# First-layer memory attention of a two-layer decoder: four-pass products replaced by three one-pass products of exact parts, with their splits, transfers and places moved

## The chip, the cores and the metric

The kernel runs on one core of a Trainium2 chip. The metric is device time in microseconds (us) of one execution; before the change the median of three runs is 2042.42 us (2042.41 to 2042.49). The span in the profile is the part of an execution between its first and last recorded instruction.

## The reference, cut to what matters

256 positions, width 2048, two layers. Layer 0 (mixer A) runs chunked gMLP gating beside a 4-head cross-attention into 256 memory tokens. The part that the change touches is that attention of layer 0:

```python
def memory_attention(q_m, mem, g_mem, w_mem_kv):
    q = q_m.reshape(B, S, MEM_HEADS, MEM_HEAD_DIM)          # 256 x 4 x 128
    kv = rmsnorm(mem, g_mem) @ w_mem_kv
    k = kv[..., :MEM_W].reshape(B, M, MEM_HEADS, MEM_HEAD_DIM)
    v = kv[..., MEM_W:].reshape(B, M, MEM_HEADS, MEM_HEAD_DIM)
    s = jnp.einsum('bshd,bmhd->bhsm', q, k) * (MEM_HEAD_DIM ** -0.5)
    p = jax.nn.softmax(s, axis=-1)
    return jnp.einsum('bhsm,bmhd->bshd', p, v).reshape(B, S, MEM_W)
# layer 0:
z = h @ w_in_a[0]          # 2048 x 3584: 1536 gate u, 1536 gate v, 512 memory queries
main = spatial_gating(z[..., :G_W], z[..., G_W:2 * G_W], ...)
x = x + concatenate([main, memory_attention(z[..., 2 * G_W:], ...)]) @ w_out[0]
```

## The kernel before, in words

**Exact parts.** Almost every product is made from two parts of each operand. A part is a `float32r` tile: the high part is the value rounded by a ScalarE copy, the low part is value minus high part, made by VectorE. Three one-pass matmuls (high x high, high x low, low x high) give the product. A few small products were left as plain `float32` matmuls, among them the scores and outputs of memory attention in both layers (`memory_scores`, `memory_out`). The trace records each such `float32` matmul as two instructions.

**Weights.** `chunk` loads a 128 x 2 x 512 piece of weights (512 KB) into a `raw` buffer on SyncE's queue (SP), then makes `whi` on ScalarE (ACT) and `wlo` on VectorE (DVE). There are four buffers of each. `gemm_fm` works on two chunks at a time, called a pair below: for both chunks all products with `whi` (L179, L180), then all with `wlo` (L182); 96 one-pass matmuls of 128x256 in all, the last 32 of them L182. After a pair, the hooks of its two chunks run: `hooks[c]` is a list of functions for chunk c. `gemm_tm` takes chunks one by one and multiplies with `whi`, `wlo`, `whi` in turn.

**Start.** `start` first makes the keys and values of layer 0 (names `kT`, `mv`, accumulated in four PSUM banks), then two GEMMs for layer 1: a `gemm_fm` of 8 chunks (hooks[0]) for the keys, and a `gemm_tm` of 8 chunks (hooks[1]) for the values. Between them, hooks evict layer 0's keys (`ek`) and values (`ev`), and `operand(h)` makes the parts of two blocks of the operand `xhl` for layer 0, h = 0 to 7. In `start`, program order is kept on PE, ACT, DVE and SP.

**Layer A.** In order: three `gemm_tm` for the v gates; one `gemm_fm` for the memory queries `qm` (with the spatial gates, L715, in hooks 4 to 7); three `gemm_fm` for the u gates, c = 0, 1, 2 with 8 chunks each, here written c0#0 to c2#7; then `w_out`. Scores of heads 0, 1 run after c0#3, those of heads 2, 3 after c0#5. The softmax result (`pm`, one 128 x 2048 tile) must be transposed. `Turn.squares` does 32x32 blocks on DVE into `small` (half of the tile at a time; the second half, `squares(8, 8)`, after c1#1), and 16 DMAs (`Turn.place`, 64 KB each) carry the blocks to their places in `pm`. `Pending.ask` spreads these 16 over the chunk loads that follow: after a load is issued on SP, `pending.some()` issues the number of places listed for it. For c = 1 and 2 program order is kept on SP. So a load behind a place on SP is not issued before that place has been. `memory_out` follows after c2#5, and `w_out` takes the four heads' blocks (12 to 15) first.

**What sets the order elsewhere.** Outside the blocks named, a scheduler sets the order in each engine's queue; PE is kept busy by the four buffers, which let loads and splits run ahead of it.

Of the kernel before, what the change touches and what calls it, by code (L numbers as in the profile page):

```python
# [101 lines left out]
class Kernel:  # L102
# [341 lines left out]
    def start(self):  # L444
# [4 lines left out]
        self.kT = [pool.tile([P, MH, S], F32, name=self.uid("kT")) for pool in (self.mk, self.cp)]  # L449
        self.mv = [pool.tile([P, 2, MW], F32, name=self.uid("mv")) for pool in (self.mk, self.cp)]  # L450
        self.rt = self.cp.tile([P, 2], F32, name="rt0")
        self.rb = self.tmp(self.cp, [P, S], "rbc", 2)
        with tc.tile_pool(name="st", bufs=1) as st:
# [48 lines left out]
            for k in range(NB):  # L502
# [29 lines left out]
                for f in hooks.get(k, ()):  # L532
# [9 lines left out]
                {  # L542
                    0: [lambda: [f() for f in late], call(operand, 5)], 1: [call(operand, 6)] + sums(self.x, xparts, 0), 2: [call(operand, 7)] + sums(self.x, xparts, 1),
                    3: sums(self.x, xparts, 2), 4: sums(self.x, xparts, 3), 5: [call(ask, "x", xparts)],
                    6: [lambda: nc.sync.dma_start(out=self.cT, in_=t["conv"]), call(columns, "x", self.rt)],
                    7: [call(rows, "x", self.rb)],
                },
# [5 lines left out]
    def memory_scores(self, l, h, q, pool, p):  # L553
        nc = self.nc
        acc = self.psum()
        for sb in range(2):
            nc.tensor.matmul(  # L557
                acc[:, sb * S : (sb + 1) * S], q[:, sb * P : (sb + 1) * P], self.kT[l][:, h, :], start=True, stop=True
            )
# [12 lines left out]
    def memory_out(self, l, h, pT, hl):  # L572
        nc, v = self.nc, self.mv[l]
        o = self.psum()
        for mb in range(2):
            nc.tensor.matmul(o[:, :S], v[:, mb, h * P : (h + 1) * P], pT[:, mb * S : (mb + 1) * S], start=mb == 0, stop=mb == 1)  # L576
        self.split(hl[:, GH + h, :], o[:, :S])


# [93 lines left out]
    def layer_a(self):  # L673
        nc, t, tc = self.nc, self.t, self.tc
        w, xhl, rt, rb = t["w_in_a"][0], self.xhl, self.rt, self.rb
        x = lambda k: xhl[:, k, :]
        ks = list(range(NB))
        with ExitStack() as ctx:
            la = ctx.enter_context(tc.tile_pool(name="la", bufs=1))
            vn = la.tile([P, 2, GW], F32, name="vn")  # L680
            vs = la.tile([P, 2, 3], F32, name="vs")

            zhooks = ({2: [lambda: self.rope_angles(la)]}, {4: [self.rope_tables]}, {})
            for c in range(3):

                def evz(tb, acc):
                    cols = slice(c * 512, (c + 1) * 512)
                    nc.scalar.activation(vn[:, tb, cols], acc, AF.Gelu, scale=rt[:, tb : tb + 1])
                    nc.scalar.activation(acc, vn[:, tb, cols], AF.Square, accum_out=vs[:, tb, c : c + 1])

                self.gemm_tm(self.rows(w, GW + c * 512, 512), NB, 512, x, evz, hooks=zhooks[c])
            vt = la.tile([P, 2], F32, name="vt")
            vr = la.tile([P, 2], F32, name="vr")
            nc.vector.tensor_reduce(vt, vs, AX.X, ALU.add)
            self.rstd(vr, vt, GW, self.cp, "rt")
            for tb in range(2):
                nc.vector.tensor_scalar(vn[:, tb, :], vn[:, tb, :], vr[:, tb : tb + 1], None, ALU.mult)

            qm = la.tile([P, MH, S], F32, name="qm")
            wT = la.tile([P, GH, P], F32, name="wT")  # L700
            bb = la.tile([P, GH, P], F32, name="bb")

            def spatial_weights():
                nc.sync.dma_start(out=bb, in_=t["b_sp"][0].rearrange("(o g) t -> o g t", o=1).to_broadcast([P, GH, P]))
                nc.sync.dma_start(out=wT, in_=t["w_sp"])
                for g in range(0, GH, 4):
                    mask = self.keep.rearrange("p (o t) -> p o t", o=1).to_broadcast([P, 4, P])
                    nc.vector.tensor_tensor(wT[:, g : g + 4, :], wT[:, g : g + 4, :], mask, ALU.mult)
# [12 lines left out]
            def eq(b, acc):
                self.scaled(qm[:, b : b + 2, :], acc, rb)
# [5 lines left out]
            pm, small = (la.tile([P, MH * 512], F32, name=name) for name in ("pm", "small"))  # L728
            turned = Turn(nc, pm, small, 4 * MH)

            def scores(h):
                view = pm[:, 512 * h : 512 * (h + 1)].rearrange("p (m a c) -> p a m c", m=2, a=2)
                self.memory_scores(0, h, qm[:, h, :], la, view)

            def out(h):
                self.memory_out(0, h, pm[:, 512 * h : 512 * (h + 1)], hl)

            each = lambda f, *hs: [lambda h=h: f(h) for h in hs]
            mhooks = {2: each(scores, 0, 1), 4: each(scores, 2, 3) + [lambda: turned.squares(0, 8)]}, {0: [lambda: turned.squares(8, 8)]}, {5: each(out, *range(MH))}
            for c in range(3):  # L740

                def eu(b, acc):
                    g = 4 * c + b
                    u = self.tmp(la, [P, 2, S], "u", 2)
                    self.scaled(u, acc, rb)
                    nc.scalar.activation(u, u, AF.Gelu)
                    u4 = u.rearrange("p g (n t) -> p g n t", n=2)
                    v4 = vn[:, :, g * P : (g + 2) * P].rearrange("p n (g t) -> p g n t", g=2)
                    nc.vector.tensor_tensor(u4, u4, v4, ALU.mult)
                    self.split_pair(hl[:, g : g + 2, :], u)  # L750

# [353 lines left out]
```

## Time and profile before

| | us |
|---|---|
| median of 3 runs | 2042.42 |
| the profiled execution | 2042.17 |
| its span | 2040.5 |
| PE busy | 2030.8 |
| DVE busy | 1362.5 |
| ACT busy | 1043.7 |

The profiled execution took 2042.17 us, 1.67 us more than its span, and lies 0.25 us under the median. PE matmuls are busy in practically the whole span. In the profile, PE is TensorE, `ps<-kT,qm` is a matmul that writes PSUM tile `ps` from `kT` and `qm`; `xN` is a count of instructions, and in the chain of waits a row gives start, duration, what and count. SPq rows are the issuing of DMAs by SyncE. An entry like `[1.90 <-DMA raw]` says that the engine sat idle so long before, and for what.

### The profile page before, as it was taken

Reading aid. Unit: us, or ns where it says so; the run is one execution under the profiler, and the core shown is the slowest. Engines: PE = TensorE matmul, PEld = TensorE weight load, DVE = VectorE, ACT = ScalarE, POOL = GpSimd, SP = SyncE. Lnnn points to the kernel's source line nnn. Section 1 sums busy time; section 2 is a strip of 40 time slices with the busy share of each in tenths; the row PEclk is TensorE's granted clock in tenths of the full one; section 3 lists DMA queues with packets and bytes.
Section 4 is the critical chain, followed back from the end, with each engine's and each line's share of the span. In section 5 each row is a group of like instructions: output and inputs, shape, how many; then the busy total and the mean of one; then the engine's idle time right before and its main releaser. Section 6 shows DMA issues by size and latency. Waiting matters only on the chain.

```text
span 2040.5 us, 38983 instructions
## 1 busy us (share of the span) xinstructions
PE 2030.8 (100%) x16200; PEld 1964.5 (96%) x16200; DVE 1362.5 (67%) x1858; ACT 1043.7 (51%) x1356; POOL 94.4 (5%) x125
## 2 busy tenths in 40 slices
PE   9999999999999999999999999999999999999998
PEld 8889999999999999999999999999988999889997
DVE  6866667767556666457689876777655667656675
ACT  6754644555435554345556674455543555434543
POOL 0000013000000000000052001200000000000000
PEclk9999999999999999999999999999999999999999
DMA  8575855666666666566665564578766666666654
GB/s 311 189 227 175 195 182 186 203 191 193 199 190 194 196 195 197 188 196 192 190 196 178 179 151 157 191 209 217 223 197 192 192 200 188 196 197 186 197 186 154
DMA packets 236753, 396.70 MB, mean 194 GB/s; under 512 B 47776, under 2 KB 54304, under 8 KB 236448
## 3 DMA queue, kind: packets, MB, share of 16 engines
q1 hardware_dynamic: 236288, 393.70, 63.0%
q8 instruction: 126, 2.06, 0.4%
q10 hardware_dynamic: 288, 0.52, 0.1%
q14 instruction: 51, 0.42, 0.1%
HBM read 387.88 MB, written 2.10 MB: 191 GB/s over the span
## 4 chain that ended last, share of the span: by engine, by line
PE 99%; DMA 0%; DVE 0%; issue 0%; ACT 0%; POOLq 0%; POOL 0%; DVEq 0%
PE ps L182 26%; PE ps L179 26%; PE ps L180 26%; PE ps L211 6%; PE ps L212 5%; PE ps L210 5%; DMA raw<-in_w_mem_kv 0%; PE ps L888 0%; PE ps L557 0%; PE ps L576 0%; PE ps L529 0%; PE ps L528 0%; PE ps L531 0%; PE ps L715 0%; PE ps L921 0%; PE ps L890 0%
## 5 line engine op out<-in xcount | busy, mean ns | idle before, releaser
L143 DVE TENSOR_TENSOR wlo<-raw,whi 128x1024 fp32r<-128x1024 f32 (+1 forms) x672 | 819.3, 1235 | 606.2 <-issue 413.7
L142 ACT ACTIVATE whi<-raw 128x1024 fp32r<-128x1024 f32 (+1 forms) x672 | 705.0, 1056 | 785.3 <-PE ps L180 569.9
L179 PE MATMUL ps<-xhl,whi 128*128 128x256 f32 x3264 | 751.2, 276 | 0.0
L180 PE MATMUL ps<-xhl,whi 128*128 128x256 f32 x3264 | 750.4, 276 | 0.0
L179 PEld LDWEIGHTS ps<-xhl,whi 128*128 128x128 f32 x3264 | 612.7, 188 | 0.2
L180 PEld LDWEIGHTS ps<-xhl,whi 128*128 128x128 f32 x3264 | 612.7, 188 | 0.2
L182 PE MATMUL ps<-xhl,wlo 128*128 128x256 f32 x3264 | 403.3, 276 | 0.0
L182 PEld LDWEIGHTS ps<-xhl,wlo 128*128 128x128 f32 x3264 | 385.2, 188 | 0.0
L179 PE MATMUL ps<-h,whi 128*128 128x256 f32 x704 | 161.6, 276 | 0.0
L180 PE MATMUL ps<-h,whi 128*128 128x256 f32 x704 | 161.5, 276 | 0.0
L631 DVE SCALAR_TENSOR_TENSOR c<-a,cT,c 128x255 f32<-128x255 f32 (+1 forms) x352 | 146.2, 478 | 0.0
L211 PE MATMUL ps<-wlo,h 128*128 128x512 f32 (+1 forms) x364 | 139.0, 382 | 0.0
L212 PE MATMUL ps<-whi,h 128*128 128x512 f32 (+1 forms) x364 | 138.7, 382 | 0.0
L210 PE MATMUL ps<-whi,h 128*128 128x512 f32 (+1 forms) x364 | 138.3, 382 | 0.0
L180 PEld LDWEIGHTS ps<-h,whi 128*128 128x128 f32 x704 | 132.0, 188 | 0.0
L179 PEld LDWEIGHTS ps<-h,whi 128*128 128x128 f32 x704 | 131.9, 188 | 0.0
L628 ACT ACTIVATE c<-a,cT 128x256 f32<-128x256 f32 x176 | 91.6, 591 | 76.8 <-DVE a L260 76.8
L179 PE MATMUL ps<-mainhl,whi 128*128 128x256 f32 x512 | 118.2, 277 | 0.0
L180 PE MATMUL ps<-mainhl,whi 128*128 128x256 f32 x512 | 117.8, 277 | 0.0
L179 PEld LDWEIGHTS ps<-mainhl,whi 128*128 128x128 f32 x512 | 95.8, 188 | 0.1
L180 PEld LDWEIGHTS ps<-mainhl,whi 128*128 128x128 f32 x512 | 95.8, 188 | 0.1
L182 PE MATMUL ps<-h,wlo 128*128 128x256 f32 x704 | 86.9, 276 | 0.0
(262 smaller groups left out, 1967.3 us busy)
## 6 DMA issues: line engine op xcount, KB each, us to landing
raw<-in_w_ffn_up SPq DMA_DIRECT2D x352, 512.0 KB, 3.9
raw<-in_w_ffn_down SPq DMA_DIRECT2D x176, 512.0 KB, 4.7
raw<-in_w_out SPq DMA_DIRECT2D x64, 512.0 KB, 4.9
raw<-in_w_in_a SPq DMA_DIRECT2D x56, 512.0 KB, 4.4
raw<-in_w_mem_kv SPq DMA_DIRECT2D x30, 512.0 KB, 5.2
raw<-in_w_in_b SPq DMA_DIRECT2D x16, 512.0 KB, 4.6
raw<-in_w_uq SPq DMA_DIRECT2D x12, 384.0 KB, 3.4
raw<-in_w_kv_a SPq DMA_DIRECT2D x8, 512.0 KB, 3.8
```

The source lines that it names most:

```text
L142: nc.scalar.activation(hi[:, :n], raw[:, :n], AF.Copy)
L143: nc.vector.tensor_tensor(lo[:, :n], raw[:, :n], hi[:, :n].bitcast(F32), ALU.subtract)
L179: mm(acc, wh, x[:, :S], start=first, stop=False)
L180: mm(acc, wh, x[:, S:], start=False, stop=False)
L182: mm(acc, wl, x[:, :S], start=False, stop=last)
L210: mm(acc, xh, wh, start=first, stop=False)
L211: mm(acc, xh, wl, start=False, stop=False)
L212: mm(acc, xl, wh, start=False, stop=last)
L628: nc.scalar.activation(c[:, i, :], a[:, i, :], AF.Identity, scale=w(2), bias=w(3))
L631: nc.vector.scalar_tensor_tensor(o, a[:, i, : S - 2 + j], w(j), o, ALU.mult, ALU.add)
```

## The change

**Operands as parts.** For layer 0, `kT` and `mv` hold high and low parts. `ek` evicts keys into a temporary `k`, and `key_parts` splits it (one ACT copy and one DVE subtraction for two blocks); `ev` makes the high part on ACT and the low part on DVE from PSUM. `eq` evicts queries into a temporary `u` and splits them. After the softmax has been transposed, `parts` splits the whole result: two ACT copies and two DVE subtractions of 128x1024. Each of the 8 score matmuls and 8 output matmuls of layer 0 becomes three.

**Places.** In `start`, evictions and splits of layer 0's keys and values are spread one to a chunk, and `operand` moves one chunk back. The spatial weights and biases, the softmax tile, its transposed squares, the queries and the softmax parts share three buffers (tags `turned`, `square`, `qm`). The 16 place DMAs begin after load c1#2 rather than c1#6, one to a load up to c2#5, then two each after c2#6 and c2#7. `memory_out` moves from c2 into `w_out`, after its chunk 3, and `w_out` takes the blocks in their order, heads last; `parts` hangs on `w_out`'s chunk 1.

```diff
-                    2: [lambda: [ev(0, tb, banks[2 + tb]) for tb in range(2)], lambda: [ek(0, 2 * b, pair(banks[b])) for b in range(2)]],
-                    **{3 + i: [call(operand, i)] for i in range(5)},
+                    2: [call(ev, 0, 0, banks[2]), call(ek, 0, 0, pair(banks[0]))],
+                    3: [call(ev, 0, 1, banks[3]), call(ek, 0, 2, pair(banks[1]))],
+                    4: [call(key_parts, 0), call(operand, 0)], 5: [call(key_parts, 2), call(operand, 1)], 6: [call(operand, 2)], 7: [call(operand, 3)],
...
+            qh, ql = q[:, cols], q[:, S + sb * P : S + (sb + 1) * P]
+            mm(o, qh, k[:, :S], start=True, stop=False)
+            mm(o, qh, k[:, S:], start=False, stop=False)
+            mm(o, ql, k[:, :S], start=False, stop=True)
...
+            hi, lo = (x[:, m] for x in pT)
+            mm(o[:, :S], v[:, mb, 0, cols], hi, start=mb == 0, stop=False)
+            mm(o[:, :S], v[:, mb, 0, cols], lo, start=False, stop=False)
+            mm(o[:, :S], v[:, mb, 1, cols], hi, start=False, stop=mb == 1)
...
+            def parts():
+                ph, pl = (self.tmp(la, [P, MH * 512], tag, 1, F32R) for tag in ("square", "qm"))
+                for h in (0, 2):
+                    cols = slice(512 * h, 512 * (h + 2))
+                    nc.scalar.activation(ph[:, cols], pm[:, cols], AF.Copy)
+                    nc.vector.tensor_tensor(pl[:, cols], pm[:, cols], ph[:, cols].bitcast(F32), ALU.subtract)
+                kept.extend((ph, pl))
...
-                    self.pending.ask(turned.places(), [0] * 6 + [2] * 8)
+                    self.pending.ask(turned.places(), [0] * 2 + [1] * 12 + [2] * 2)
...
-            self.w_out(0, hl, [12, 13, 14, 15] + list(range(12)))
+            self.w_out(0, hl, list(range(NB)), {1: [parts], 3: each(out, *range(MH))})
```

**SP, the u gates.** Here are the loads c1#2 to c1#7 (the rows with `raw`) with the first places in SP's queue, before the change:

```order
L132 DMA raw_2322<-in_w_in_a 128x2x512
L132 DMA raw_2328<-in_w_in_a 128x2x512
L132 DMA raw_2382<-in_w_in_a 128x2x512
L132 DMA raw_2388<-in_w_in_a 128x2x512
L132 DMA raw_2442<-in_w_in_a 128x2x512
L96 DMA pm<-small 32x16x32 x2
L132 DMA raw_2450<-in_w_in_a 128x2x512
```

and with the change:

```order
L132 DMA raw_2352<-in_w_in_a 128x2x512
L96 DMA turned_1966<-square_1967 32x16x32
L132 DMA raw_2359<-in_w_in_a 128x2x512
L96 DMA turned_1966<-square_1967 32x16x32
L132 DMA raw_2414<-in_w_in_a 128x2x512
L96 DMA turned_1966<-square_1967 32x16x32
L132 DMA raw_2421<-in_w_in_a 128x2x512
```

The first place has moved ahead of four loads: c1#3 (`raw_2359`), c1#4, c1#5 and c1#6 now stand behind it.

**DVE, the same stage.** From the maxima of heads 2, 3 to the first splits of c1; `STREAM_TRANSPOSE` is `Turn.squares`, the second one `squares(8, 8)`. Before (`wlo_2324` is c1#2, `wlo_2330` c1#3, `wlo_2384` c1#4):

```order
L568 RECIPROCAL den_2166<-den_2166 128x2
L143 TENSOR_TENSOR wlo_2324<-raw_2322,whi_2323 128x1024
L568 RECIPROCAL den_2178<-den_2178 128x2
L260 TENSOR_TENSOR u_2245<-ps_1954,rbc_97 128x512
L260 TENSOR_TENSOR u_2251<-ps_1955,rbc_97 128x512
L143 TENSOR_TENSOR wlo_2330<-raw_2328,whi_2329 128x1024
L91 STREAM_TRANSPOSE small<-pm 128x8x4x32
L749 TENSOR_TENSOR u_2245<-u_2245,vn 128x512
```

With the change (`wlo_2354` is c1#2, `wlo_2361` c1#3):

```order
L143 TENSOR_TENSOR wlo_2354<-raw_2352,whi_2353 128x1024
L591 RECIPROCAL den_2208<-den_2208 128x2
L260 TENSOR_TENSOR u_2275<-ps_1968,rbc_97 128x512
L260 TENSOR_TENSOR u_2281<-ps_1969,rbc_97 128x512
L91 STREAM_TRANSPOSE square_1967<-turned_1966 128x8x4x32
L791 TENSOR_TENSOR u_2275<-u_2275,vn 128x512
L791 TENSOR_TENSOR u_2281<-u_2281,vn 128x512
L270 TENSOR_TENSOR mainhl_1965<-u_2275,mainhl_1965 128x2x256
L270 TENSOR_TENSOR mainhl_1965<-u_2281,mainhl_1965 128x2x256
L143 TENSOR_TENSOR wlo_2361<-raw_2359,whi_2360 128x1024
```

The split of c1#3 has moved from ahead of the second transposition to behind it and behind the gating of c0.

**DVE, the start.** Splits of layer 1's key weights, chunks 4 to 7, and of the first value chunk (called t0; `wlo_868` before, `wlo_872` now), with what stands between them. Before:

```order
L260 TENSOR_TENSOR kT_92<-ps_106,mrb 128x512
L260 TENSOR_TENSOR kT_92<-ps_107,mrb 128x512
L275 SCALAR_TENSOR_TENSOR xhl_90<-xT,gT,xhl_90 128x256 x2
L148 SCALAR_TENSOR_TENSOR wlo_722<-raw_720,gT,whi_721 128x512 x2
L148 SCALAR_TENSOR_TENSOR wlo_730<-raw_728,gT,whi_729 128x512 x2
L275 SCALAR_TENSOR_TENSOR xhl_90<-xT,gT,xhl_90 128x256 x4
L148 SCALAR_TENSOR_TENSOR wlo_794<-raw_792,gT,whi_793 128x512 x2
L148 SCALAR_TENSOR_TENSOR wlo_802<-raw_800,gT,whi_801 128x512 x2
L275 SCALAR_TENSOR_TENSOR xhl_90<-xT,gT,xhl_90 128x256 x4
L148 SCALAR_TENSOR_TENSOR wlo_868<-raw_866,gT,whi_867 128x512 x2
```

With the change, from the first eviction to chunk 6:

```order
L504 SCALAR_TENSOR_TENSOR mv_94<-ps_108,mrt,mv_94 128x512
L260 TENSOR_TENSOR k_81_714<-ps_106,mrb 128x512
L504 SCALAR_TENSOR_TENSOR mv_94<-ps_109,mrt,mv_94 128x512
L260 TENSOR_TENSOR k_82_718<-ps_107,mrb 128x512
L148 SCALAR_TENSOR_TENSOR wlo_722<-raw_720,gT,whi_721 128x512 x2
L148 SCALAR_TENSOR_TENSOR wlo_730<-raw_728,gT,whi_729 128x512 x2
L270 TENSOR_TENSOR kT_92<-k_81_714,kT_92 128x2x256
L275 SCALAR_TENSOR_TENSOR xhl_90<-xT,gT,xhl_90 128x256 x2
L270 TENSOR_TENSOR kT_92<-k_82_718,kT_92 128x2x256
L275 SCALAR_TENSOR_TENSOR xhl_90<-xT,gT,xhl_90 128x256 x2
L148 SCALAR_TENSOR_TENSOR wlo_798<-raw_796,gT,whi_797 128x512 x2
```

Two low parts of values and two of keys have come in ahead of the later splits, and two of the ten `xhl` operations that stood ahead of t0 now stand behind the value chunk t3 (the last `operand`).

More of the change, by code (lines that the diff above doesn't have):

```diff
@@ L448, in start @@
         mhl = self.ap.tile([P, NB, 512], F32R, tag="big", name=self.uid("memhl"))
-        self.kT = [pool.tile([P, MH, S], F32, name=self.uid("kT")) for pool in (self.mk, self.cp)]
-        self.mv = [pool.tile([P, 2, MW], F32, name=self.uid("mv")) for pool in (self.mk, self.cp)]
+        self.kT = [self.mk.tile([P, MH, 2 * S], F32R, name="kT0"), self.cp.tile([P, MH, S], F32, name="kT1")]
+        self.mv = [self.mk.tile([P, 2, 2, MW], F32R, name="mv0"), self.cp.tile([P, 2, MW], F32, name="mv1")]
         self.rt = self.cp.tile([P, 2], F32, name="rt0")
@@ L483, in rows, with key_parts @@
                 self.row_rstd(rb, kept[name + "d"])
+            k0 = {}
             def ek(l, b, acc):
-                self.scaled(self.kT[l][:, b : b + 2, :], acc, mrb)
-            def ev(l, tb, acc):
-                nc.scalar.activation(self.mv[l][:, tb, :], acc, AF.Copy, scale=mrt[:, tb : tb + 1])
+                if l == 1:
+                    self.scaled(self.kT[1][:, b : b + 2, :], acc, mrb)
+                    return
+                k0[b] = self.tmp(st, [P, 2, S], "k0", 2)
+                self.scaled(k0[b], acc, mrb)
+            def key_parts(b):
+                self.split_pair(self.kT[0][:, b : b + 2, :], k0[b])
+            def ev(l, tb, acc):
+                r = mrt[:, tb : tb + 1]
+                if l == 1:
+                    nc.scalar.activation(self.mv[1][:, tb, :], acc, AF.Copy, scale=r)
+                    return
+                hi, lo = self.mv[0][:, tb, 0, :], self.mv[0][:, tb, 1, :]
+                nc.scalar.activation(hi, acc, AF.Copy, scale=r)
+                nc.vector.scalar_tensor_tensor(lo, acc, r, hi.bitcast(F32), ALU.mult, ALU.subtract)
             m = lambda k: mhl[:, k, :]
@@ L538, in start @@
                     1: [call(rows, "m", mrb)],
-                    2: [lambda: [ev(0, tb, banks[2 + tb]) for tb in range(2)], lambda: [ek(0, 2 * b, pair(banks[b])) for b in range(2)]],
-                    **{3 + i: [call(operand, i)] for i in range(5)},
-                },
-                {
-                    0: [lambda: [f() for f in late], call(operand, 5)], 1: [call(operand, 6)] + sums(self.x, xparts, 0), 2: [call(operand, 7)] + sums(self.x, xparts, 1),
-                    3: sums(self.x, xparts, 2), 4: sums(self.x, xparts, 3), 5: [call(ask, "x", xparts)],
+                    2: [call(ev, 0, 0, banks[2]), call(ek, 0, 0, pair(banks[0]))],
+                    3: [call(ev, 0, 1, banks[3]), call(ek, 0, 2, pair(banks[1]))],
+                    4: [call(key_parts, 0), call(operand, 0)], 5: [call(key_parts, 2), call(operand, 1)], 6: [call(operand, 2)], 7: [call(operand, 3)],
+                },
+                {
+                    0: [lambda: [f() for f in late], call(operand, 4)], 1: [call(operand, 5)] + sums(self.x, xparts, 0),
+                    2: [call(operand, 6)] + sums(self.x, xparts, 1),
+                    3: sums(self.x, xparts, 2) + [call(operand, 7)], 4: sums(self.x, xparts, 3), 5: [call(ask, "x", xparts)],
                     6: [lambda: nc.sync.dma_start(out=self.cT, in_=t["conv"]), call(columns, "x", self.rt)],
@@ L555, in memory_scores @@
         acc = self.psum()
+        mm, k = nc.tensor.matmul, self.kT[l][:, h, :]
         for sb in range(2):
-            nc.tensor.matmul(
-                acc[:, sb * S : (sb + 1) * S], q[:, sb * P : (sb + 1) * P], self.kT[l][:, h, :], start=True, stop=True
-            )
+            o, cols = acc[:, sb * S : (sb + 1) * S], slice(sb * P, (sb + 1) * P)
+            if l == 1:
+                mm(o, q[:, cols], k, start=True, stop=True)
+                continue
+            qh, ql = q[:, cols], q[:, S + sb * P : S + (sb + 1) * P]
+            mm(o, qh, k[:, :S], start=True, stop=False)
+            mm(o, qh, k[:, S:], start=False, stop=False)
+            mm(o, ql, k[:, :S], start=False, stop=True)
         scale = 128 ** -0.5
@@ L573, in memory_out @@
         nc, v = self.nc, self.mv[l]
+        mm, cols = nc.tensor.matmul, slice(h * P, (h + 1) * P)
         o = self.psum()
         for mb in range(2):
-            nc.tensor.matmul(o[:, :S], v[:, mb, h * P : (h + 1) * P], pT[:, mb * S : (mb + 1) * S], start=mb == 0, stop=mb == 1)
+            m = slice(mb * S, (mb + 1) * S)
+            if l == 1:
+                mm(o[:, :S], v[:, mb, cols], pT[:, m], start=mb == 0, stop=mb == 1)
+                continue
+            hi, lo = (x[:, m] for x in pT)
+            mm(o[:, :S], v[:, mb, 0, cols], hi, start=mb == 0, stop=False)
+            mm(o[:, :S], v[:, mb, 0, cols], lo, start=False, stop=False)
+            mm(o[:, :S], v[:, mb, 1, cols], hi, start=False, stop=mb == 1)
         self.split(hl[:, GH + h, :], o[:, :S])
@@ L697, in layer_a @@
                 nc.vector.tensor_scalar(vn[:, tb, :], vn[:, tb, :], vr[:, tb : tb + 1], None, ALU.mult)
-            qm = la.tile([P, MH, S], F32, name="qm")
-            wT = la.tile([P, GH, P], F32, name="wT")
-            bb = la.tile([P, GH, P], F32, name="bb")
+            qm = self.tmp(la, [P, MH * 512], "qm", 1, F32R).rearrange("p (h c) -> p h c", h=MH)
+            wT, bb = (self.tmp(la, [P, MH * 512], tag, 1)[:, :GW].rearrange("p (g t) -> p g t", g=GH) for tag in ("turned", "square"))
             def spatial_weights():
@@ L721, in eq @@
             def eq(b, acc):
[L722 removed]
+                q = self.tmp(la, [P, 2, S], "u", 2)
+                self.scaled(q, acc, rb)
+                self.split_pair(qm[:, b : b + 2, :], q)
             hooks = {1: [spatial_weights], **{4 + i: [lambda i=i: gates(3 * i)] for i in range(4)}}
@@ L727, in layer_a @@
             hl = self.ap.tile([P, NB, 512], F32R, tag="big", name=self.uid("mainhl"))
-            pm, small = (la.tile([P, MH * 512], F32, name=name) for name in ("pm", "small"))
+            pm, small = (self.tmp(la, [P, MH * 512], tag, 1) for tag in ("turned", "square"))
             turned = Turn(nc, pm, small, 4 * MH)
@@ L733, in scores @@
                 self.memory_scores(0, h, qm[:, h, :], la, view)
+            kept = []
+            def parts():
[5 more added lines that the diff above has]
+                kept.extend((ph, pl))
             def out(h):
-                self.memory_out(0, h, pm[:, 512 * h : 512 * (h + 1)], hl)
+                self.memory_out(0, h, [x[:, 512 * h : 512 * (h + 1)] for x in kept], hl)
             each = lambda f, *hs: [lambda h=h: f(h) for h in hs]
-            mhooks = {2: each(scores, 0, 1), 4: each(scores, 2, 3) + [lambda: turned.squares(0, 8)]}, {0: [lambda: turned.squares(8, 8)]}, {5: each(out, *range(MH))}
+            mhooks = {2: each(scores, 0, 1), 4: each(scores, 2, 3) + [lambda: turned.squares(0, 8)]}, {0: [lambda: turned.squares(8, 8)]}, {}
             for c in range(3):
```

## The prediction

> **What bounds the kernel now.** I read the page first (busy shares and the chain that ended last), then who waits for whom on PE, then the chain of waits where the change acts, then SP's and DVE's timelines there.
>
> ```profile
> span 2040.5 us, 38983 instructions
> PE 2030.8 (100%) x16200; PEld 1964.5 (96%) x16200; DVE 1362.5 (67%) x1858; ACT 1043.7 (51%) x1356; POOL 94.4 (5%) x125
> PE 99%; DMA 0%; DVE 0%; issue 0%; ACT 0%; POOLq 0%; POOL 0%; DVEq 0%
> ```
>
> The first row is the span, the second busy time by engine, the third the chain by engine: it is PE from end to end. All that PE waits for, from the view of waits:
>
> ```profile
> PE ps L329 <- DVE ones L318: 1.1, 1, 1.1
> PE ps L179 <- ACT whi L164: 0.5, 1, 0.5
> PE ps L211 <- DVE wlo L148: 0.2, 1, 0.2
> ```
>
> So no stall is left to remove: 1.8 us in all, most of it at the first instruction. The time can fall only by the passes that PE is spared, and rises by every wait that the change puts in front of PE. The chain of waits shows what the memory heads cost there (start, duration, what, count):
>
> ```profile
> 197.97 1.82 PE ps L182 x16
> 199.78 1.73 PE ps L557 x8
> 205.18 1.82 PE ps L182 x16
> 207.00 1.73 PE ps L557 x8
> 212.39 1.81 PE ps L182 x16
> 217.83 1.81 PE ps L182 x16
> ...
> 250.47 1.81 PE ps L182 x16
> 252.29 3.45 PE ps L576 x16
> ```
>
> Sixteen one-pass matmuls take 1.81 us, 0.113 each. L182 x16 rows end a pair, and 217.83 - 212.39 = 5.44 us is a pair, 2.72 a chunk. A four-pass matmul is two records: four score matmuls (x8) take 1.73, eight output matmuls (x16) 3.45, so 0.431 each.
>
> **The change part by part.**
>
> **Passes.** Eight score and eight output matmuls go: 1.73 + 1.73 + 3.45 = 6.91 us. Forty-eight one-pass ones of 128x256 come: 48 x 0.113 = 5.43. PE gains 1.5 us. New weight loads stand beside matmuls, as they do in the pairs.
>
> **Start.** DVE gets two low parts of values, read from PSUM, and two of keys, all 128x512. The trace has neither, but it has their neighbours:
>
> ```profile
> 70.06 1.41 DVE L148 SCALAR_TENSOR_TENSOR wlo<-raw,gT,whi 128x512 fp32r<-128x512 f32 x2
> 72.50 1.29 DVE L260 TENSOR_TENSOR kT<-ps,mrb 128x512 f32<-128x512 f32 x2 [1.04 <-PE ps L182]
> 73.71 0.87 DVE L275 SCALAR_TENSOR_TENSOR xhl<-xT,gT,xhl 128x256 fp32r<-128x256 f32 x2
> 74.50 1.41 DVE L148 SCALAR_TENSOR_TENSOR wlo<-raw,gT,whi 128x512 fp32r<-128x512 f32 x2
> 82.33 1.40 DVE L148 SCALAR_TENSOR_TENSOR wlo<-raw,gT,whi 128x512 fp32r<-128x512 f32 x2
> 72.75 0.40 PE L210 MATMUL ps<-whi,memhl 128*128 128x512 f32 x1
> 75.50 0.39 PE L210 MATMUL ps<-whi,memhl 128*128 128x512 f32 x1
> 83.66 0.39 PE L210 MATMUL ps<-whi,memhl 128*128 128x512 f32 x1
> ```
>
> The first, fourth and fifth rows are the splits of value chunks t0, t1 and t4; the PE rows are those chunks' first matmuls. A 128x512 operation costs 0.65 from L148 (half of 1.41, less some overlap) to 0.60 from L260: four make 2.5 us. Two `xhl` operations leave, 0.8 (73.71 to 74.50). DVE reaches t0 1.7 late, at 71.8; its first half is ready 0.7 later, at 72.5. PE wants it one matmul after 72.75, that is at 72.98 (12 matmuls between 72.75 and 75.50, 0.23 each): no stall. DVE's 1.04 of idle at 72.50 then takes up most of the delay, and 0.7 stays. t1: ready at 74.50 + 0.7 + 0.7 = 75.9, wanted at 75.73: 0.17 late. The two displaced `xhl` operations stand ahead of t4: ready at 82.33 + 0.7 + 0.8 + 0.7 = 84.5, wanted at 83.66 + 0.23 + 0.17 = 84.06: 0.45 more. I take 0.6 us. The ends are 0 (no work leaves PE's path here, so no gain) and 1.7, the whole delay. The two ACT copies for the keys stand beside this, ahead of splits that are wanted a pair later.
>
> **The first place.** SP issues in order. From its timeline, the loads c1#2, c1#3, then c1#4 and c1#5, c1#6, then the first two places, then c1#7; below them SP's wait, two rows of DVE and one of ACT:
>
> ```profile
> 200.22 0.37 SPq L132 DMA_DIRECT2D raw<-in_w_in_a  x1
> 201.35 0.37 SPq L132 DMA_DIRECT2D raw<-in_w_in_a  x1
> 208.14 3.67 SPq L132 DMA_DIRECT2D raw<-in_w_in_a  x2
> 214.62 0.37 SPq L132 DMA_DIRECT2D raw<-in_w_in_a  x1
> 218.13 1.41 SPq L96 DMA_DIRECT2D pm<-small  x2
> 219.59 0.62 SPq L132 DMA_DIRECT2D raw<-in_w_in_a  x1
> SPq L96 <- DVE small L91: 3.1, 1, 3.1
> 215.74 1.21 DVE L143 TENSOR_TENSOR wlo<-raw,whi 128x1024 fp32r<-128x1024 f32 x1
> 216.87 1.23 DVE L91 STREAM_TRANSPOSE small<-pm 128x1024 f32<-128x1024 f32 x1
> 224.85 1.06 ACT L142 ACTIVATE whi<-raw 128x1024 fp32r<-128x1024 f32 x1 [1.90 <-DMA raw<-in_w_in_a]
> ```
>
> Before, SP reaches the first place after c1#6 and still waits 3.1 us for the second transposition, which ends at 218.1. Now it reaches that place right after c1#2, near 200.6, and load c1#3, issued at 201.35 before, stands behind it. The transposition itself comes sooner: the split of c1#3, which was ahead of it, is now behind (1.13 from 215.74 to 216.87), and the first score groups are 0.37 shorter. It ends near 216.6. One place costs half of 218.13 to 219.59, 0.73, so c1#3 is issued at 217.4, 16 us later than before.
>
> When does it land? The DMA view of 195 to 218 (no places) and of 218 to 242 (with them) gives queue packets, MB and share, and at the end of a row the median us to landing:
>
> ```profile
> q1 hardware_dynamic: 1900, 3.66, 50.1%
> raw<-in_w_in_a SPq DMA_DIRECT2D x7, 512.0 KB, 3.7
> ...
> q1 hardware_dynamic: 10221, 4.75, 102.3%
> raw<-in_w_in_a SPq DMA_DIRECT2D x9, 512.0 KB, 7.2
> pm<-small SPq DMA_DIRECT2D x16, 64.0 KB, 6.7
> ```
>
> Seven loads fill 50.1% of 23 us, 1.65 each. Of the second window's 4.75 MB the places are 1.05, so 7.1 loads passed, 11.7 of 24.5 us of queue time, and 16 places had the other 12.8: 0.8 each. The ends for c1#3 are 3.7 and 7.2. The nearest row is c1#7, issued at 219.59 behind two places, for which ACT waited until 224.85: 5.26. With one place less, 4.45. So c1#3 lands at 221.85 and its high part is ready after 1.06, at 222.9. PE's pair c1#2, c1#3 began at 217.83 + 1.81 = 219.64; its first 1.81 us need c1#2 alone; the shorter scores bring it 0.74 forward: wanted at 220.7. PE stalls 2.2 us (1.4 with a landing of 3.7, 4.9 with one of 7.2). [...]
>
> **The other loads, and the parts.** Behind c1#3 a load with one place needs 1.65 + 0.8 = 2.45 us of the queue, PE 2.72 a chunk, so the lead grows again. c2#7 comes six pairs later, 32.6 us of PE. Until it, 12 loads and 13 places pass: 30.2 us. But ACT's two copies in `parts` (2.1 us, as two splits of that size) stand ahead of c2#7's split in ACT's queue and wait for the sixteenth place, two places (1.6) behind that load: 33.9 against 32.6, 1.3 us late. With a load's cost 7% lower they would be just in time. I take 0.6, ends 0 and 1.3. Output matmuls of the heads and their splits come 48 one-pass matmuls and more before `w_out` uses blocks 12 to 15, as ahead of pairs before: nothing. Query splits (two operations each on ACT and DVE) fall behind the query GEMM, whose last splits are done pairs before the scores want `qm`: nothing, since 10.9 us of PE (two pairs) stand between; without that cover they would cost 1.2, two of 0.60.
>
> **Sum.** -1.5 + 0.6 + 2.2 + 0.6 = +1.9 us on the profiled execution's 2042.17: 2044.1. It lies 0.25 under the median of 2042.42, so 2044.3.
>
> **The rivals.**
>
> *No wait, passes alone.* The transposition ends earlier, or c1#3 lands so soon that four buffers hide it, and DVE's slack hides the start: 2042.42 - 1.5 = 2040.9. For it: before, SP held 3 us of lead. Against it: c1#3's issue is tied to a DVE operation 4 us before PE wants the data, and even a landing of 3.7 leaves 1.4.
>
> *The stall decides.* Place: c1#3 alone. It shares the queue with places issued behind it and lands after 7.2, the median of that window: a stall of 4.9, 2042.42 - 1.5 + 0.6 + 4.9 + 0.6 = 2047.0, slower by 0.22%. The point is a landing of 6.7. If PE's clock, 1.00 in every slice here, were halved for one pair after so long an idle time, that is 5.44 more, 2052.5. [...] Against this rival: only one place is ahead of the load, in an idle queue.
>
> *The products are not one-pass.* With 0.431 for each of 48, +13.8 us: 2056. The same tile type and shape runs at 0.113 throughout, so this is very unlikely.
>
> **How the numbers follow.** The forecast has 0.65, passes alone 0.20, the decisive stall 0.12, products that stay four-pass 0.01, a gain that I don't see 0.02. A measurement of this kernel can tell about 0.2%, 4.1 us, from no change: 2038.3 to 2046.5 is the same. Faster 0.02, same 0.85, slower 0.13. The range goes from passes alone, 2040.7, to the stall's end, 2047.2; the forecast's own is 2042.3 to 2046.
>
> **What would show it.** Scores x12 in 1.36 us and outputs x24 in 2.72. SP's place waiting some 16 us for `square`. A wait of PE L179 for ACT's `whi` near 220 of about 2 us, none over 3; small waits of L211 for DVE's `wlo` near 76 and 84; one at the end of c2, near 256, of at most 1.3. I am wrong if PE waits at none of these, if c1#3 is late by 5, or if the chain leaves PE elsewhere.

## The result, and the profile after

The changed kernel takes 2046.07 us, the median of 17 runs (2044.20 to 2049.08), against 2042.41 of the kernel before in as many runs. One of those 17 took 2929.28 us, for which nothing here gives a cause, and is left out of the ratio. The ratio is 1.0018, with a 95% interval of 1.0011 to 1.0024: 3.7 us more, 0.18%. That is little, but every run of the changed kernel lies above the other 16 of the kernel before, which end at 2043.03. The time lay 1.8 us above the forecast and inside the whole range, 0.07 above the end of the forecast's own. The 17 runs fall into three groups: four at 2044.2 to 2044.85, eleven at 2045.75 to 2046.71, two at 2048.7 and 2049.1. The profiled execution took 2048.68 and belongs to the last group, with all losses in it.

From the page of the changed kernel: the span, busy time by engine, the chain that ended last by engine.

```profile
span 2047.0 us, 39033 instructions
PE 2035.3 (99%) x16216; PEld 1968.9 (96%) x16216; DVE 1368.7 (67%) x1866; ACT 1048.7 (51%) x1362; POOL 94.4 (5%) x125
PE 97%; DVE 2%; DMA 1%; issue 0%; ACT 0%; SPq 0%; POOLq 0%; POOL 0%; DVEq 0%; ACTq 0%
```

Two things differ from before. DVE and DMA have gained a share of the chain, so somewhere PE waited for them. Most of DVE's 2% is the start, where the chain runs over DVE from 57 to 84 us. And PE is busy for 4.5 us longer although it has less to do, so it was also slower. The view of waits (us in total, times, longest) names the stall; its third row is SP's own wait, between 150 and 300 us, and names what lies behind it:

```profile
PE ps L179 <- ACT whi L142: 2.3, 1, 2.3
PE ps L211 <- DVE wlo L148: 0.2, 1, 0.2
SPq L96 <- DVE square L91: 15.8, 1, 15.8
```

SP stands 15.8 us at the first place, waiting for the second transposition, with the load of c1#3 behind it. The chain of waits of the changed kernel shows what follows (start, duration, what):

```profile
213.62 1.23 DVE wlo L143
214.92 1.19 DVE u L260 x2
216.10 1.17 DVE square L91
217.33 0.75 SPq L96
218.13 4.74 DMA raw<-in_w_in_a
222.96 1.06 ACT whi L142
224.07 0.58 PE ps L179
224.65 0.21 PE ps L180
...
233.48 1.92 PE ps L182 x16
239.24 1.92 PE ps L182 x16
...
273.80 1.92 PE ps L182 x16
282.15 1.81 PE ps L182 x16
```

The path leaves PE and runs through the transposition, the place, c1#3's load and its split, and back to PE at 224.07. Behind that two things stand out. A matmul takes 0.21 us instead of 0.113. And later pairs are still slow: sixteen L182 take 1.92 us, 0.120 each, until 273.80; from 282.15 they are back at 1.81. The windows view gives, for each stretch, its length, the busy time and count of PE, PEld, DVE, ACT and POOL, and then the granted clock, the DMA share and GB/s:

```profile
217.20:220.60 3.40, 3.40 (x33) 3.40 (x32) 2.65 (x5) 2.37 (x4) 0.00 (x0) 1.00 0.31 57
220.60:224.00 3.40, 1.14 (x11) 0.94 (x9) 0.00 (x0) 1.04 (x1) 0.00 (x0) 1.00 1.08 326
224.00:227.40 3.40, 3.33 (x15) 3.33 (x16) 2.45 (x2) 1.43 (x3) 0.00 (x0) 0.50 1.08 296
227.40:230.80 3.40, 3.40 (x31) 3.40 (x29) 1.57 (x2) 1.77 (x2) 0.00 (x0) 1.00 1.15 242
```

PE was busy for 1.14 of 3.40 us (the second row). In the next 3.40 us the clock was halved, and 15 matmuls were done where 31 are done in the row after. From there the clock is full again, 1.00 from 227.5 to 275.7, so the 0.120 us of a matmul in that stretch (404 matmuls in 48.2 us) isn't a lower granted clock.

With these the three groups can be built from terms that the traces show: 0.75 more at the start and 1.22 less for the products (both are worked out below), 2.33 of stall: 2042.4 + 1.9 = 2044.3, the first group. With the halved clock, 15 to 16 matmuls by 0.10, 1.6 more: 2045.9, the second. With about 400 matmuls at 0.120 in place of 0.113, 2.7 more: 2048.6, the third.

### The profile page after: what moved, and what is told of

Its sections match the earlier page's. It is cut to its first block, busy times and chain, and to the rows that moved or that the text cites. A ratio compares the mean times of both kernels' runs of the same rounds, so it can differ in the third digit from the quotient of the medians.

```text
span 2047.0 us, 39033 instructions
## 1 busy us (share of the span) xinstructions
PE 2035.3 (99%) x16216; PEld 1968.9 (96%) x16216; DVE 1368.7 (67%) x1866; ACT 1048.7 (51%) x1362; POOL 94.4 (5%) x125
## 4 chain that ended last, share of the span: by engine, by line
PE 97%; DVE 2%; DMA 1%; issue 0%; ACT 0%; SPq 0%; POOLq 0%; POOL 0%; DVEq 0%; ACTq 0%
PE ps L179 26%; PE ps L180 26%; PE ps L182 26%; PE ps L211 5%; PE ps L212 5%; PE ps L210 5%; DVE wlo L148 1%; DMA raw<-in_w_mem_kv 0%; PE ps L930 0%; PE ps L544 0%; PE ps L543 0%; PE ps L546 0%; DVE xhl L275 0%; PE ps L745 0%; PE ps L963 0%
## 5 line engine op out<-in xcount | busy, mean ns | idle before, releaser
L182 PE MATMUL ps<-xhl,wlo 128*128 128x256 f32 x3264 | 404.0, 276 | 0.0
L182 PEld LDWEIGHTS ps<-xhl,wlo 128*128 128x128 f32 x3264 | 385.9, 188 | 0.0
L211 PE MATMUL ps<-wlo,h 128*128 128x512 f32 (+1 forms) x364 | 139.0, 382 | 0.0
L210 PE MATMUL ps<-whi,h 128*128 128x512 f32 (+1 forms) x364 | 138.3, 382 | 0.0
L182 PE MATMUL ps<-h,wlo 128*128 128x256 f32 x704 | 86.9, 276 | 0.0
```

Source lines behind the costliest of these rows:

```text
L182: mm(acc, wl, x[:, :S], start=False, stop=last)
L210: mm(acc, xh, wh, start=first, stop=False)
L211: mm(acc, xh, wl, start=False, stop=False)
```

## Experiments: the stall and the clock

All ratios are to the kernel before, run on the same chip in the same series; its median was 2042.5 to 2042.6 in each.

**The order alone, without the products.** The kernel before, with only the counts of places per load changed to nearly those of the change:

```diff
-                    self.pending.ask(turned.places(), [0] * 6 + [2] * 8)
+                    self.pending.ask(turned.places(), [0] * 2 + [1] * 8 + [2] * 4)
```

> The kernel before, with four-pass products, and only the first place moved ahead to behind c1#2 (one to a load for eight loads, then two for four). Theory A: PE idles at c1#3 some 2.8 us (the second transposition 0.5 us later than in the changed kernel, PE 0.7 later), the clock drops in most runs: 2042.4 + 2.8 = 2045.2 without the drop, 2047 to 2050 with it. Theory B: 2042.4.

Measured: 2045.40 (2044.74 to 2048.00, 11 runs), ratio 1.0016 [1.0007, 1.0025].

```profile
PE ps L179 <- ACT whi L142: 2.3, 1, 2.3
222.00:224.00 2.00, 0.15 (x2) 0.00 (x0) 0.00 (x0) 0.70 (x1) 0.00 (x0) 1.00 1.09 325
224.00:226.00 2.00, 1.59 (x7) 1.59 (x8) 1.23 (x1) 1.10 (x2) 0.00 (x0) 0.53 1.11 314
226.00:228.00 2.00, 2.00 (x13) 2.00 (x12) 1.23 (x1) 1.21 (x2) 0.00 (x0) 0.62 1.14 315
```

The same stall and the same half clock behind it, in a kernel that has none of the new products. Six runs lie at 2044.7 to 2045.4, which is the stall alone (2042.5 + 2.3 = 2044.8); five at 2046.5 to 2048.0, with a lower mean clock. So the place ahead of load c1#3 makes both. The stall was shorter than the 2.8 expected.

**The same data, the idle time filled.** The change, with 20 one-pass matmuls of no use put ahead of c1#3's first matmul. Loads and splits stay as they are, so PE can't go on any sooner:

```diff
+            if n == len(jobs) // 2:
+                for _ in range(fill):
+                    mm(spare[:, :S], jobs[0][1], jobs[0][3][:, :S], start=True, stop=True)
...
-            self.mm_fm(jobs)
+            self.mm_fm(jobs, fill if c0 == 2 else 0)
```

> The changed kernel with 20 one-pass matmuls more, whose result nothing reads, ahead of PE's first matmul with c1#3: they fill the idle time with 2.27 us of work. Theory A1 (the loss behind the wait comes from the clock, which drops because PE idled): no half clock, no 120 ns; only the wait itself is lost, 2044.2 in all runs, with little spread. Theory A2 (matmuls at 120 ns come from the transfers or the new buffers, not from the idle time): 2.7 us more, 2047, in the runs that had it before.

Measured: 2045.01 (2044.16 to 2046.96, 11 runs), ratio 1.0013 [1.0005, 1.0022]. The windows view of this kernel:

```profile
222.00:224.00 2.00, 2.00 (x20) 2.00 (x19) 0.00 (x0) 1.04 (x1) 0.00 (x0) 1.00 1.10 310
224.00:226.00 2.00, 2.00 (x19) 2.00 (x18) 1.23 (x1) 0.64 (x2) 0.00 (x0) 1.00 1.10 298
```

Busy throughout, the clock stays at 1.00, and none of the 11 runs shows a lowered mean clock (13 of 17 of the change do). With 2.3 us of useless work the median is 1.1 us below that of the change without it. But not all runs came to 2044.2 as expected: four lie at 2045.7 to 2047.0, with the full clock. That was a second loss, taken up below.

**Less filling, and a longer stall.** Eight such matmuls in place of 20 leave an idle time of 1.4 us. And two places ahead of c1#3's load in place of one:

```diff
-                    self.gemm_fm(..., hooks=mhooks[c], fill=20 if c == 1 else 0)
+                    self.gemm_fm(..., hooks=mhooks[c], fill=8 if c == 1 else 0)
```

> The change with 8 one-pass matmuls of no use (0.9 us) put ahead of c1#3's first matmul, so that PE idles 1.4 us in place of 2.3; data and loads as in the change. Theory (length of the idle time): no drop of the clock, 2044.2 to 2045.2, as with 20 such matmuls. Rival (any stall here, by chance): the drop in most runs, 2046.

```diff
-                    self.pending.ask(turned.places(), [0] * 2 + [1] * 12 + [2] * 2)
+                    self.pending.ask(turned.places(), [0] * 2 + [2] + [1] * 13 + [1])
```

> The change with two places ahead of c1#3's load in place of one. The stall grows by one place on SP and the queue, 0.7 to 0.8, to 3.1: 2044.85 in runs with the clock kept, 2046.6 in runs with the drop. Theory (the drop depends on how long PE was idle): the drop in nearly all runs, more than the 13 of 17 of the change. Rival (any stall at this place may drop the clock, by chance): 3 in 4, as in the change.

Measured: with 8 matmuls 2044.49 (2044.18 to 2044.79), ratio 1.0009 [1.0000, 1.0018]; with two places 2046.56 (2044.81 to 2047.10), ratio 1.0017 [1.0009, 1.0026]. The waits of the first, then the wait and two windows of the second:

```profile
PE ps L183 <- ACT whi L142: 1.4, 1, 1.4
```

```profile
PE ps L179 <- ACT whi L142: 2.8, 1, 2.8
224.00:226.00 2.00, 1.16 (x8) 1.16 (x9) 1.18 (x1) 1.21 (x2) 0.00 (x0) 0.90 1.08 316
226.00:228.00 2.00, 2.00 (x12) 2.00 (x11) 1.27 (x2) 1.06 (x2) 0.00 (x0) 0.50 1.10 275
```

| longest wait of PE in the profile behind the first instruction, us | runs with a lowered clock |
|---|---|
| at most 0.4 (20 matmuls, two kernels) | 0 of 22 |
| 1.4 (8 matmuls) | 0 of 11 |
| 2.3 (order alone) | 5 of 11 |
| 2.3 (the change) | 13 of 17 |
| 2.8 (two places) | 8 of 11 |

The last column counts the runs whose mean granted clock is 0.998 where the others have 0.999: 3.41 us at half speed take 0.0008 off it. From 1.4 to 2.3 us of idle the count goes from none of 11 to 18 of 28, with 2.8 to 8 of 11: up to 2.3 the length matters, and from there on chance as well, whose source no run shows. That nearly all runs would drop with two places wasn't borne out: 8 of 11 is the share of the change, as the rival had it, and the stall grew to 2.8 only, not to 3.1. The useless work of 0.9 us thus brought the whole group at 2046 down to 2044.5. In the change, the half clock lasts from 224.013 to 227.426, 3.41 us. For the other two the clocks of the 2 us windows give it as an estimate: 224.12 to 227.52 with the order alone (0.53 and 0.62), 225.60 to 229.04 with two places (0.90, 0.50, and 0.74 from 228 to 230), about 3.4 us each. With two places that is some 0.8 us after PE has gone on (at 224.84), with the order alone 0.3 us before (224.41), with the change 0.06 before (224.07). So the drop doesn't follow the idle time at a fixed distance, and what sets its start isn't shown. In the 3.41 us ahead of the drop PE was idle for 2.27 (change) and, by the estimated starts, 1.96 (order alone) and 2.65 us (two places): some 2.0 us were enough here. No run tried idle times between 1.4 and 2.3. (The kernel with late places, below, had a lowered mean clock in 3 of 11 runs; its profiled run had a wait of 0.8 us and no drop, and how long PE idled in those three isn't known.)

## Experiments: the order of places, and who else was late

**All places late,** and **the first place one load later:**

```diff
-                    self.pending.ask(turned.places(), [0] * 2 + [1] * 12 + [2] * 2)
+                    self.pending.ask(turned.places(), [0] * 6 + [2] * 8)
```

> The changed kernel with the 16 places issued as before the change (two to a load, from c1#6 on). Theory A (the first place, now ahead of load c1#3, makes PE idle 2.3 us, and the idle time makes the clock drop): no wait of PE at c1#3, no half clock, no matmuls at 120 ns; 2042.4 - 1.5 for the passes + 0.7 for the start = 2041.6. Theory B (the extra splits, the shared buffers or the parts cost the time): still 2044 to 2046.

```diff
-                    self.pending.ask(turned.places(), [0] * 2 + [1] * 12 + [2] * 2)
+                    self.pending.ask(turned.places(), [0] * 3 + [1] * 10 + [2] * 3)
```

> The changed kernel with the first place one load later, behind c1#3 instead of c1#2 (then one to a load, two behind each of the last three). Theory A: the delayed load is now c1#4, whose pair starts 3.6 us after PE wants c1#3; its high part is ready near 224.0, PE wants it near 223.5, so an idle time of 0.5 us or less, too short for the clock to drop: 2041.6 to 2042.2. Theory B: as the changed kernel, 2044 to 2046.

Measured: late 2044.56 (2042.37 to 2047.07), ratio 1.0011 [1.0002, 1.0020]; one load later 2042.65 (2042.41 to 2044.43), ratio 1.0002 [0.9993, 1.0011]. The stall at c1#3 is gone in both; the first expectation was missed by 3 us, the second by 0.45. ACT's and PE's timelines of the kernel with late places say why:

```profile
243.96 2.01 ACT L773 ACTIVATE square<-turned 128x1024 fp32r<-128x1024 f32 x2 [5.57 <-DMA raw<-in_w_in_a]
245.87 1.14 ACT L788 ACTIVATE u<-u 128x512 f32<-128x512 f32 x2
246.91 1.99 ACT L142 ACTIVATE whi<-raw 128x1024 fp32r<-128x1024 f32 x2
248.01 0.39 PE L179 MATMUL ps<-xhl,whi 128*128 128x256 f32 x1 [0.84 <-ACT whi L142]
```

L773 is `parts`. ACT stood idle for 5.57 us in front of it, though splits of loads that had landed were queued behind it, and PE waited for one of these, c2#4. `parts` needs the last place, and what stood behind `parts` didn't start before it; so the last place, not a load, held ACT. The profile names a load as what ended the wait, but the two splits at 246.91, of loads that had landed, needed no further wait. In the kernel with 20 matmuls of no use (its lines are numbered four higher) the same row stands ahead of c2#7's split:

```profile
252.40 2.01 ACT L777 ACTIVATE square<-turned 128x1024 fp32r<-128x1024 f32 x2 [5.61 <-DMA turned<-square]
254.31 3.89 ACT L142 ACTIVATE whi<-raw 128x1024 fp32r<-128x1024 f32 x4
255.41 0.39 PE L183 MATMUL ps<-xhl,whi 128*128 128x256 f32 x1 [0.23 <-ACT whi L142]
```

**`parts` behind.** Tied to a value that c2's last eviction writes, `parts` must stand behind c2#7's split and the first splits of `w_out`. First in the kernel with 20 matmuls:

```diff
+                one = self.tmp(la, [P, 1], "one", 1)
+                nc.vector.tensor_scalar(one, hl[:, 11, S - 1 : S].bitcast(F32), 0.0, 1.0, ALU.mult, ALU.add)
...
-                    nc.scalar.activation(ph[:, cols], pm[:, cols], AF.Copy)
+                    nc.scalar.activation(ph[:, cols], pm[:, cols], AF.Copy, scale=one)
```

> The order of the change with 20 one-pass matmuls of no use in the idle time, as one run before, whose times lay from 2044.16 to 2046.96 without a drop of the clock, and parts tied behind c2's last eviction. Theory (ACT held by parts makes that spread: the last place lands by chance earlier or later, and PE is not slowed here): all runs at 2044.2 to 2044.8. Rival (the spread is PE's own, 120 ns a matmul, or late loads): runs up to 2047 as before.

Measured: 2044.86 (2044.05 to 2045.27), ratio 1.0011 [1.0002, 1.0019]. The runs near 2046 and 2047, four of 11, are gone in 11 runs, so the spread was most likely `parts`. The median fell by 0.15 only, and is somewhat above the 2044.2 to 2044.8 expected.

**One load later, and the start changed; then `parts` behind as well.**

```diff
-                    4: [call(key_parts, 0), call(operand, 0)], 5: [call(key_parts, 2), call(operand, 1)], ...
+                    4: [call(operand, 0)], 5: [call(operand, 1)], ...
...
-                    3: sums(self.x, xparts, 2) + [call(operand, 7)], ...
+                    3: sums(self.x, xparts, 2), ...
+                    6: [..., call(columns, "x", self.rt), call(operand, 7)],
+                    7: [call(rows, "x", self.rb), call(key_parts, 0), call(key_parts, 2)],
```

> The order with the first place behind c1#3, and the start mended: the two splits of the keys stand behind the row sums of x, operand 7 behind the column sums. Theory: the start's 0.75 us adds to the rest as it stood, so 0.75 below the same order with the start as the change has it (2042.65): 2041.9, and the splits of t1 and t4 let PE go on without a wait near 76 and 84. Rival: the start's delay is made up later by loads that wait, or the key splits do the same harm where they now stand: 2042.6 and a wait near 90.

> As the run before it, and the two copies of parts are tied to a value that the last eviction of c2 writes, so that they stand behind c2#7's split and the splits of w_out's first chunks on ACT. Theory: what is above the passes alone (2042.5 - 1.5 = 2041.0) is ACT held by parts until the last place lands; it goes, 2041.0 to 2041.2, and runs lie within 0.5 us of one another. Rival: it is the queue of loads and places itself, which stays: as the run before, 2041.9, and PE waits for a high part at the end of c2 whose DMA was late.

Measured: 2042.93 (2042.19 to 2043.50), ratio 1.0001 [0.9992, 1.0010]; with `parts` behind 2042.48 (2042.16 to 2043.18), ratio 1.0001 [0.9992, 1.0009]. The start was not mended: the row below, the same in both kernels, is at t7, where the kernel before had 0.2, and it costs what was saved at t1 and t4. The rival had a wait near 90 right, but not its cause: operand 7, put behind the column sums, stands in program order right ahead of t7's split on DVE (two such operations take 0.87 us, as in the kernel with all moved below; PE idles 0.96 for that split in both). With `parts` behind, the median fell by 0.45, within the spread of the runs, and no wait at the end of c2 is left; but the time didn't come to 2041. A place ahead of c1#4's load still makes PE late by 0.1 to 0.2 at several matmuls between 224.8 and 227.4, 0.46 in all, too short for the view of waits to list.

```profile
PE ps L211 <- DVE wlo L148: 1.0, 1, 1.0
```

**All moved.** The first place behind c1#4 (`[0] * 4 + [1] * 11 + [5]`, the last five behind c2#7), `parts` behind; with the operands of x moved back, two fewer of them ahead of t1's split and the last one in layer A, and the same with the start as the change has it:

```diff
-                    4: [call(key_parts, 0), call(operand, 0)], 5: [call(key_parts, 2), call(operand, 1)], 6: [call(operand, 2)], 7: [call(operand, 3)],
+                    4: [call(key_parts, 0)], 5: [call(key_parts, 2)], 6: [call(operand, 0)], 7: [call(operand, 1)],
...
+                    0: [lambda: [f() for f in late], call(operand, 2)], 1: [call(operand, 3)] + sums(self.x, xparts, 0),
+                    2: [call(operand, 4)] + sums(self.x, xparts, 1),
+                    3: sums(self.x, xparts, 2), 4: sums(self.x, xparts, 3) + [call(operand, 5)], 5: [call(ask, "x", xparts)],
+                    6: [lambda: nc.sync.dma_start(out=self.cT, in_=t["conv"]), call(operand, 6), call(columns, "x", self.rt)],
...
+            self.operand7 = call(operand, 7)
...
+            zhooks = ({0: [self.operand7], 2: [lambda: self.rope_angles(la)]}, {4: [self.rope_tables]}, {})
```

> The one-pass products, with no wait left as far as the traces name them: the first place behind load c1#4, one place per load, the last five behind c2#7; parts tied behind c2's last eviction; two operands of x (0.8 us of DVE each) fewer ahead of the split of t1, and one fewer behind it, ahead of t4. Theory (the four-pass matmuls were worth 1.5 us and all else is waits that the order makes): PE waits only as the kernel before does, 1.8 us; 2042.55 - 1.5 = 2041.05, faster than before by 0.07%, in all runs within 0.5. Rival (some of the loss cannot be ordered away, as queue time of places or DVE time in the start): between 2041.5 and 2042.5.

> As the run before it, but with the start as the change has it. The prediction's term for the start was 0.6, the trace of the change shows 0.75: 2041.8, with waits of 0.16 at t1 and 0.29 at t4. Rival (the delay of the start is caught up later): as the run before it.

Measured: 2041.98 (2041.45 to 2042.47), ratio 0.9996 [0.9987, 1.0005]; with the old start 2042.06 (2041.89 to 2042.73), ratio 0.9997 [0.9988, 1.0006]. The order of places costs nothing any more: from c1#0 on, ten pairs in a row take 5.44 us in both. Neither reached what was expected, 2041.05 and 2041.8; both lie where the first one's rival had it, 2041.5 to 2042.5. The median of the kernel with the old start lies 0.49 below that of the kernel before, which the interval doesn't tell from nothing, but it is what the products bring (1.22, see below) less what the start costs (0.75). The other shows why moving the operands gained next to nothing (DVE and PE, around the column sums):

```profile
89.78 0.87 DVE L275 SCALAR_TENSOR_TENSOR xhl<-xT,gT,xhl 128x256 fp32r<-128x256 f32 x2
90.57 0.15 DVE L284 TENSOR_SCALAR rtv<-ps 128x2 f32<-128x2 f32 x1
92.96 1.41 DVE L148 SCALAR_TENSOR_TENSOR wlo<-raw,gT,whi 128x512 fp32r<-128x512 f32 x2
93.76 0.50 PE L211 MATMUL ps<-wlo,memhl 128*128 128x512 f32 x1 [0.60 <-DVE wlo L148]
```

An operand stands ahead of `rtv`, which starts a chain of nine short operations, and t7's split stands behind that chain.

**Three operands out of the second half.**

```diff
-            self.operand7 = call(operand, 7)
+            self.rest = [call(operand, i) for i in (5, 6, 7)]
...
-            zhooks = ({0: [self.operand7], 2: ...
+            zhooks = ({0: self.rest[:2], 1: self.rest[2:], 2: ...
```

> As the run with all moved, but three operands of x (2.4 us of DVE) leave the second half of the start altogether; they stand in the first GEMM of the memory, between the splits of its chunks. There the last operand stood ahead of the column sums and delayed them and the split of t7: PE waited 0.6 where the kernel before waits 0.2. Theory (the start's loss is DVE's order alone): waits at t1, t4 and t7 as in the kernel before, 2042.55 - 1.5 = 2041.05 at best, 0.5 to 0.9 below the run with the old start (2042.06). Rival (DVE is as full in the first GEMM): a wait of PE L179 for the split of L164 or L165 there, above the 0.5 us of before, and 2041.5 to 2042.

In the program the three stand in layer A, behind all of the start. The scheduler, which sets the order there, has DVE do them far ahead, in the first GEMM of the memory:

```profile
33.83 0.87 DVE L275 SCALAR_TENSOR_TENSOR xhl<-xT,gT,xhl 128x256 fp32r<-128x256 f32 x2
38.69 1.67 DVE L275 SCALAR_TENSOR_TENSOR xhl<-xT,gT,xhl 128x256 fp32r<-128x256 f32 x4
```

Measured: 2041.22 (2040.94 to 2041.63, 11 runs), against 2042.54 (2042.33 to 2043.09, 15 runs) of the kernel before: ratio 0.9993, interval 0.9984 to 1.0002. The interval holds 1, but all 11 runs lie below all 15, so I take it to be faster by 1.3 us. All waits of PE, and the chain around the products, where the score rows between the pairs are left out:

```profile
span 2039.4 us, 39035 instructions
PE ps L329 <- DVE ones L318: 1.1, 1, 1.1
PE ps L211 <- DVE wlo L148: 0.2, 1, 0.2
```

```profile
198.09 1.82 PE ps L182 x16
...
204.98 1.82 PE ps L182 x16
...
266.27 1.81 PE ps L182 x16
...
274.62 1.81 PE ps L182 x16
```

Nothing but the start's own two waits is left. (The 0.5 for L164 that the kernel before shows isn't among them, but it is no part of the gain: t0 starts at 72.89 here and at 72.75 before.) From one pair to the next with the scores of two heads between, PE needs 6.89 us where it needed 7.21 (205.18 - 197.97). With the four outputs between, it needs 8.35. Before, the L182 row behind the outputs is this one of the chain, 8.93 after the one at 250.47:

```profile
259.40 1.81 PE ps L182 x16
```

The products are thus worth 0.32 + 0.32 + 0.58 = 1.22 us; the medians differ by 1.32, the spans of the two profiled executions by 1.1.

## Why the prediction was right or wrong

**The sum without the clock: right, in part by luck.** It came to 1.9; the traces give -1.22 + 0.75 + 2.33 = 1.86. Passes, start and stall were each put down too low, by 0.56 together, and the 0.6 for `parts` made up for it.

**Passes: right, a little too large a gain.** 1.22 in place of 1.5. The products' matmuls take 0.12 rather than 0.113: the scores of two heads 6.89 - 5.44 = 1.45 and the outputs 8.35 - 5.44 = 2.91, in place of 1.36 and 2.72. (5.44 us are 48 matmuls at 0.113. So a pair is 48 matmuls, 16 of them L182, and not 96 and 32 as the words on `gemm_fm` have it; the prediction went by the 5.44.)

**Start: right.** The terms were 0.17 at t1 and 0.45 more at t4. PE's timeline of the changed kernel:

```profile
75.67 0.39 PE L210 MATMUL ps<-whi,memhl 128*128 128x512 f32 x1
76.06 0.50 PE L211 MATMUL ps<-wlo,memhl 128*128 128x512 f32 x1
84.17 0.39 PE L210 MATMUL ps<-whi,memhl 128*128 128x512 f32 x1
84.69 0.50 PE L211 MATMUL ps<-wlo,memhl 128*128 128x512 f32 x1
```

Between L210 and L211 0.23 is normal; here it is 0.39 and 0.52, that is 0.16 and 0.29 late, and the matmul behind each late one starts 0.1 later still (0.33 behind it). From t0 (72.93, before 72.75) to the L182 row ahead of the scores (198.89, before 197.97) PE lost 0.75, against 0.6 foreseen. That this is the order of DVE is shown by the last kernel, which has none of it.

**The first place: right in place, mechanism and size.** SP waited for the transposition 15.8 us ("some 16"); it ended at 217.3 (216.6); the load landed 4.74 after its issue (4.45); the stall was 2.33 (2.2). That PE and DVE both come some 0.9 later here (198.89 for 197.97) moves both ends of the stall alike.

**`parts` and c2#7: right in mechanism, unseen in the profiled execution.** It predicted 0 to 1.3 and took 0.6. The profile of the change shows no wait there: behind the stall PE had come another 3.8 us late, by the half clock and the slow matmuls (L182 of c2#6, c2#7 at 262.28 rather than 258.5), so the split was there in time. The four runs with the full clock lie at most 0.6 above the sum without `parts`. In the kernel with 20 matmuls the wait is there, 0.23 in the profile, and it goes when `parts` is moved.

**What failed: the clock.** The sum had no term for it. It was named, as an addition to the rival of a 4.9 us stall and at 5.44 us a time; the term for a stall of 2.2 was zero, though the longest wait of PE before was 1.1 and no wait showed what one of 2.2 does. (And the 1.00 put down for every slice doesn't hold at the very end: behind PE's last matmul, which ends at 2032.65, the clock of before is 0.50 from 2034.95 on.) The runs showed a drop in 13 of 17 runs at 2.3 us of idle, worth 1.6. Had it stood in the sum at that, the forecast would have been 2045.9 against 2046.07. The drop is much cheaper than the pair at half speed that was put down (5.44), as it lasts 3.41 us.

**Also unforeseen: 0.120 us a matmul** for 48 us after the half clock, in the profiled execution and, by its time alone, in one more of the 17 runs. Its cause stays open; no other profile caught it. The run of the order alone at 2048.0, 1.1 above the next, has no profile either.

## What to carry to other kernels

Price a stall of TensorE with the clock behind it: here an idle time of 2.3 us cost 1.6 more in 18 of 28 runs, one of 1.4 in none of 11, and filling it with useless matmuls won the difference back. A transfer that waits for a late result held everything behind it in SyncE's ordered queue for 15.8 us here, and a copy that waited for the last such transfer held what stood behind it on ScalarE for 5.57 us: count loads and splits that stand behind it before spreading transfers "one per load". A gain of 1.2 us in passes came out in full only when three orders (places, `parts`, operands) had been put right, and each was found by asking what the idle engine stood in front of, not who was busy.

## What the runs showed of the hardware that I had not expected

- The granted clock was halved for 3.41 us in the change (about 3.4 by estimate in two more kernels) after 2.0 to 2.65 us of idle within the 3.41 us ahead; no run of 33 in which filling left 1.4 us or less showed a lowered mean clock. The drop came between 0.3 us before and 0.8 us after PE had gone on.
- After one such drop PE ran for 48 us at 0.120 us a matmul with a granted clock of 1.00; a pair elsewhere takes 5.44 us, 0.113 a matmul.
- Matmuls of the small products between two pairs start 0.12 apart, not 0.113, at the full clock.
